# An encoder with 32 experts per layer: down weights in a ring of their own, one more megabyte ahead, row operations on GpSimd

## The chip, the core and the metric

The kernel runs on one core of a Trainium2 chip. The metric is the device time of one execution in microseconds (us); the time before is the median of three runs. A profile of one further execution shows what each engine and each DMA queue did. Engines are TensorE (PE; its weight loads as PEld), VectorE (DVE), ScalarE (ACT), GpSimd (POOL) and SyncE (SP), which here only issues transfers.

## What is computed

A trunk of two layers over 256 tokens of width 1024, all in float32. Each layer mixes tokens by four branches behind one input projection and then runs a mixture of 32 experts, of which each token takes two:

```python
h = layer_norm(x, emb_ln_g, emb_ln_b)
for l in range(DEPTH):                                   # 2 layers
    mix = token_mixing(h, ...)                           # 4 branches, gates, output projection
    h = layer_norm(ALPHA * h + mix, ln1_g[l], ln1_b[l])
    ffn = hierarchical_moe(h, ...)                       # top-1 group, then top-2 experts of 32
    h = layer_norm(ALPHA * h + ffn, ln2_g[l], ln2_b[l])

def expert_block(xb, e):
    return (silu(xb @ w_gate[e]) * (xb @ w_up[e])) @ w_down[e]   # 1024x512, 1024x512, 512x1024
```

Every expert's three matrices are 2 MB each (a megabyte, MB, is 2^20 bytes where tiles are counted), so a layer reads 192 MB for its experts, whatever the tokens choose.

## The kernel before

**Weights as a stream.** `weight_sources` lists every weight of both layers in the order of use. `load_weight` takes the next megabyte of that list and loads it, on SyncE's queue, into a buffer of the pool that it is given; `take` hands a source's tiles out, and its `free(i)` calls `load_weight` with the pool of the buffer just used up. So a freed buffer at once asks for the next megabyte, and the requests go out in the order in which SyncE's program has them. A request waits for the engine that last read the buffer.

**The buffers.** A buffer holds 128 partitions of 8 KB, 1 MB. `rawp` has 8 for the whole run. `rawb` has 4 and is opened late in the mixing (at the third branch). In the expert stage the space of the mixing's split weights becomes a further ring: `open_ring`, a step of the hand-written order in `output_and_route`, opens `rawc` with 5 buffers and loads them. `rawd` adds one when routing has ended. That is 18 megabytes ahead of the first expert. Only `rawp` may load for the next layer: for the other pools `load_weight` returns (L186).

**An expert's tiles.** The gate and up weights of an expert are four tiles (kind "pair": a half of gate, a half of up, and again), the down weight two (kind "down", 1 MB each, 8 KB pieces), listed one expert later than its pair, as it is used. The last expert's down weight comes as two column halves of four small transfers each (kind "halves").

**The expert loop** (`moe`, L926 to L965). For each expert p there are twelve steps s. Steps 0 to 7 are the gate and up products of p, two tiles in steps 0 to 3 and two in steps 4 to 7; each pair of tiles is freed after its fourth step. Steps 8 to 11 are the down product of expert p-1, each tile freed after two steps. Between them, by the table `STEPS`, stand the evacuation of p's products (`evacuate`, after step 7), their transposes, silu, and `combine` of p-2 in step 9, and `weigh` of p-1 in step 11; gathers of the next four experts' tokens stand in step 9 too. After the loop the last expert's down product runs by halves, and the layer norm follows. The order on each engine is as written there (`manual_schedule`).

**Small tiles.** `t4` has 6 buffers of 4 KB per partition, `t2` 8 buffers of 2 KB. The selection matrices `g` of the gathers stand in `t4`.

**The start.** The two rows of the embedding norm (`load_rows`) are turned into columns by TensorE and copied by ScalarE (`turn_rows`, L311 to L318). `enter_mixing` computes the norm's statistics, issues `FILL[0]` = 28 filling products on TensorE (`keep_busy`, L356; each is two passes in the trace), normalises and transposes. `turn_rows` stands outside the part whose order is written by hand.

**The whole-row operations.** `finish_h` (L380 to L385) multiplies the normalised rows by the norm's gain and adds its offset, two operations for each of two row tiles of 128x1024, on VectorE, in the mixing of each layer. The next reader is the residual addition after the output product.

Of the kernel before, what the change touches and what calls it, by code (L numbers as in the profile page):

```python
# [10 lines left out]
F32 = mybir.dt.float32  # L11
# [18 lines left out]
FILL = (28, 16)  # L30
G = 2
# [75 lines left out]

class Kernel:
# [19 lines left out]
    def open_ring(self):  # L128

        self.close_side()  # L130
        self.side = [self.tc.tile_pool(name=f"rawc{self.layer}", bufs=RAW[2] * 2 // G + 1, side="right", reuse_waits="tile")]
        self.rawc, = (p.__enter__() for p in self.side)
        for _ in range(RAW[2] * 2 // G + 1):
            self.load_weight(self.rawc)

    def close_side(self):
        for p in self.side[::-1]:
            p.__exit__(None, None, None)
        self.side, self.rawc = [], None
# [6 lines left out]
    def weight_sources(self):  # L146
        a = self.a
        for l in range(self.depth):
            w = a["w_in"][l].rearrange("(k p) c -> p k c", p=128)
            d = COL_DIL  # L150

            def cols(*starts, w=w):
                return [(w[:, :, s:s + 256], 256) for s in starts]

            yield l, [(w[:, :, d:d + 512], 512)]
            yield l, [(w[:, :, d + 768:d + 1280], 512)]
            yield l, [(w[:, :, d + 1536:d + 2048], 512)]
            yield l, cols(d + 512, d + 1280)
            yield l, cols(d + 2048, 512)
            yield l, [(w[:, :, 0:512], 512)]  # L160
            yield l, [(w[:, :, COL_DIFF:COL_DIFF + 512], 512)]
            yield l, [(w[:, :, COL_DIFF + 512:COL_DIFF + 1024], 512)]
            yield l, [(a["const_big"][:, :2048].rearrange("p (k c) -> p k c", k=4), 512)]
            wb = a["w_branch"][l]
            for n in BRANCH_ORDER:
                for h in range(2):
                    s = COL_GATE + n * D + h * 512
                    yield l, [(w[:, :, s:s + 512], 512)]
                yield l, [(wb[n].rearrange("(k p) d -> p k d", p=128), 1024)]
            wo = a["w_out"][l].rearrange("(k p) d -> p k d", p=128)  # L170
            for h in range(2):
                yield l, [(wo[:, :, h * 512:(h + 1) * 512], 512)]
            for e in range(N_EXP + 1):
                if e < N_EXP:
                    yield l, [(a[name][l, e].rearrange("(f p k) c -> p f k c", f=2, k=4), 512)
                              for name in ("expert_w_gate", "expert_w_up")], "pair"
                if e:
                    src = a["expert_w_down"][l, e - 1].rearrange("(h p k) d -> p h k d", h=2, k=2)
                    yield l, [(src, D)], "halves" if e == N_EXP else "down"

    def load_weight(self, pool):
# [4 lines left out]
        if self.ahead is None or (pool in (self.rawb, self.rawc, self.rawd) and self.ahead[0] > self.layer):  # L186
            return
# [4 lines left out]
        if kind:  # L192
# [6 lines left out]
            elif kind == "down":  # L199
                t = pool.tile([128, 2, 2, 512], F32, tag="raw", name="raw")  # L200
                nc.sync.dma_start(t.rearrange("p k f c -> p k (f c)"), blocks[0][0][:, q])
            else:
                t = pool.tile([128, 4, 2, 256], F32, tag="raw", name="raw")
                src = blocks[0][0].rearrange("p h k (f i c) -> p h k f i c", f=2, i=2)
                for k in range(4):
                    nc.sync.dma_start(t[:, k], src[:, k // 2, k % 2, :, q])
# [13 lines left out]
        if self.part == parts:  # L220
            self.ahead = None

# [157 lines left out]
    def finish_h(self, *v):  # L380

        g, b = (self.broadcast(x) for x in v)
        for T in range(2):
            self.nc.vector.tensor_mul(self.h[T], self.h[T], g)
            self.nc.vector.tensor_add(self.h[T], self.h[T], b)  # L385


    def run(self):
        tc, nc, a = self.tc, self.nc, self.a
        with ExitStack() as ctx:  # L390
# [3 lines left out]
            self.rawb = self.rawc = self.rawd = None  # L394
# [20 lines left out]
            for n, w in CONST:  # L415
# [5 lines left out]
            self.turn_rows(self.load_rows([a[n].rearrange("(o d) -> o d", o=1) for n in ("emb_ln_g", "emb_ln_b")], 1,  # L421
                                          nc.scalar), 0)
# [15 lines left out]
            with tc.manual_schedule():  # L438
                for T in range(2):
# [356 lines left out]
    def moe(self, l):  # L796
        tc, nc, a, c = self.tc, self.nc, self.a, self.c
        mm, t2, t4, t8 = self.mm, self.t2, self.t4, self.t8
        with ExitStack() as ctx:
# [9 lines left out]
            def slots(e0, T):  # L809

                if T == 0:
                    gs[e0] = t4.tile([128, 2, batch, CAP], F32R, tag="t4", name="g")
# [61 lines left out]
            def evacuate(e):  # L874
                st["h", e] = t2.tile([128, 512], F32, tag="t2", name="hid")
                nc.scalar.copy(st["h", e].rearrange("q (h k p) -> q h p k", h=2, k=2),  # L876
                               gu.rearrange("q (h p k) -> q h p k", h=2, k=2))
# [45 lines left out]
            with tc.manual_schedule():  # L923
                self.load_weight(self.rawd)
                nc.vector.tensor_copy(meta[:, :, :, 1], gates)
                for p in range(N_EXP):  # L926
# [4 lines left out]
                    for s in range(12):  # L931
                        if s == 0:
                            tiles, _, free = self.take() if p else ahead
                        if s == 8 and p:
                            tiles, _, free = self.take()
# [19 lines left out]
                        elif p:  # L955
                            down(p - 1, s - 8, tiles[s // 2 - 4][:, s % 2], dn)
                            if s % 2:
                                free(s // 2 - 4)
# [104 lines left out]
    def output_and_route(self, l, rp, route, meta, slots, gather, gathered, begin):  # L1063
# [180 lines left out]
        bks(1)  # L1244
        starts(0, 1)
# [78 lines left out]
    def overflow(self, l, rp, route, sel, gates, count, xh, xl, acc):  # L1324
# [17 lines left out]
        with tc.For_i(0, n, 1):  # L1342
# [18 lines left out]
            xs = t4.tile([128, 8, CAP], F32, tag="t4", name="oxs")  # L1361
# [68 lines left out]
```

## Time and profile before

| | us |
|---|---|
| median of 3 runs (lowest to highest) | 1532.85 (1529.71 to 1535.23) |
| the profiled execution | 1530.08 |
| its span, first to last instruction | 1528.0 |
| TensorE busy | 1467.8 (96%) |
| VectorE, ScalarE busy | 571.0, 468.7 |
| GpSimd busy | 0.2 (4 memsets) |
| HBM read | 498.65 MB, 328 GB/s over the span |

The share of busy time is a mean over stages with different limits. The first layer's mixing runs to about 314 us, its experts from there to about 756, the second layer's mixing to about 1063 and its experts to about 1507; the last norm and the output end the span. A busy TensorE is not one at its peak, since the ends of its products are modelled.

### The profile page before, as it was taken

What the parts mean: (1) busy time and instruction counts of PE and PEld (TensorE: products, weight loads), DVE (VectorE), ACT (ScalarE), POOL (GpSimd) and SP (SyncE); (2) the same over time, 40 slices, a digit from 0 to 9 for tenths busy, and PEclk for the clock granted to TensorE, in tenths of its full rate; (3) what the DMA queues carried; (4) which work ended last, traced back from release to release, by engine and by line L of the source; (5) the groups of instructions that cost most, each with busy time, mean ns of one, the idle gap of its engine ahead of it and who ended that gap; (6) DMA issues with size and microseconds to landing.
All of it is one profiled execution on the core that took longest, in us unless ns stands there. A gap on an engine that the chain in (4) does not pass through costs nothing. (4 is left out here: it accounts for less than half of the span.)

```text
span 1528.0 us, 21590 instructions
## 1 busy us (share of the span) xinstructions
PE 1467.8 (96%) x8848; PEld 896.1 (59%) x8848; DVE 571.0 (37%) x1202; ACT 468.7 (31%) x764; POOL 0.2 (0%) x4
## 2 busy tenths in 40 slices
PE   8989999999999999999899999999999999999995
PEld 7777899844444444444378778997444444444432
DVE  5477765721111111111176766665111111111103
ACT  5445555521111111111264555454111111111111
POOL 0000000000000000000000000000000000000000
PEclk9989999999999999999999999999999999999998
DMA  9744485679999999999988336746999999999996
GB/s 334 230 167 138 136 303 195 249 306 419 420 420 419 420 420 419 419 420 421 391 246 308 111 111 214 252 167 254 395 420 420 419 420 420 419 420 420 421 420 217
DMA packets 121658, 501.16 MB, mean 328 GB/s; under 512 B 23050, under 2 KB 35786, under 8 KB 72660
## 3 DMA queue, kind: packets, MB, share of 16 engines
q1 hardware_dynamic: 121248, 499.14, 83.8%
q8 instruction: 72, 1.18, 0.3%
q10 hardware_dynamic: 308, 0.60, 0.1%
q14 instruction: 30, 0.25, 0.0%
HBM read 498.65 MB, written 2.00 MB: 328 GB/s over the span
## 5 line engine op out<-in xcount | busy, mean ns | idle before, releaser
L854 PE MATMUL bank<-raw,xs 128*64 128x512 f32 x2048 | 481.7, 595 | 20.0 <-DMA raw<-in_expert_w_up_dram 19.9
L854 PEld LDWEIGHTS bank<-raw,xs 128*64 128x64 f32 x2048 | 166.3, 137 | 302.2 <-issue 239.5
L896 PE MATMUL bank<-raw,act 128*64 128x512 f32 (+1 forms) x1056 | 261.0, 586 | 0.0
L239 DVE TENSOR_TENSOR wl<-raw,wh 128x1024 fp32r<-128x1024 f32 x159 | 192.6, 1222 | 113.7 <-ACT wh L234 110.0
L876 ACT COPY hid<-bank 128x512 f32<-128x512 f32 x64 | 68.3, 1067 | 457.9 <-PE bank L854 457.9
L234 ACT CAST wh<-raw 128x1024 fp32r<-128x1024 f32 x159 | 165.6, 1050 | 136.6 <-PE mm L484 60.6
L831 DVE COPY xs<-bank 128x256 f32<-128x256 f32 x116 | 43.9, 420 | 421.9 <-PE bank L822 421.9
L484 PE MATMUL mm<-hth,wh 128*128 128x256 f32 x576 | 162.8, 283 | 0.0
L484 PE MATMUL mm<-hth,wl 128*128 128x256 f32 x576 | 162.4, 282 | 0.0
L484 PE MATMUL mm<-htl,wh 128*128 128x256 f32 x576 | 162.2, 282 | 0.0
L896 PEld LDWEIGHTS bank<-raw,act 128*64 128x64 f32 x1056 | 78.4, 136 | 130.8 <-issue 124.6
L908 DVE SCALAR_TENSOR_TENSOR y<-bank,tg,y 128x512 fp32r<-128x512 f32 (+1 forms) x66 | 48.5, 735 | 178.0 <-ACT y L907 178.0
L484 PEld LDWEIGHTS mm<-hth,wh 128*128 128x128 f32 x576 | 109.1, 189 | 2.4 <-issue 2.2
L484 PEld LDWEIGHTS mm<-htl,wh 128*128 128x128 f32 x576 | 109.2, 190 | 1.1 <-issue 0.8
L484 PEld LDWEIGHTS mm<-hth,wl 128*128 128x128 f32 x576 | 109.1, 189 | 1.0 <-issue 0.8
L907 ACT ACTIVATE y<-bank,tg 128x512 fp32r<-128x512 f32 (+1 forms) x66 | 44.5, 674 | 166.2 <-PE bank L896 166.2
L465 PE MATMUL mm<-wh,hth 128*128 128x512 f32 x220 | 72.7, 402 | 1.0 <-ACT hth L300 1.0
L465 PE MATMUL mm<-wl,hth 128*128 128x512 f32 x220 | 71.7, 401 | 0.0
L465 PE MATMUL mm<-wh,htl 128*128 128x512 f32 x220 | 70.2, 398 | 0.0
L822 PEld LDWEIGHTS bank<-g,xh 128*128 128x128 f32 x240 | 36.9, 192 | 50.9 <-issue 50.9
L888 ACT ACTIVATE act<-bank 128x256 f32<-128x256 f32 x64 | 24.6, 385 | 127.7 <-PE bank L882 125.5
L822 PE MATMUL bank<-g,xh 128*128 128x256 f32 x240 | 55.0, 311 | 3.7 <-DVE g L813 3.7
(228 smaller groups left out, 1453.6 us busy)
## 6 DMA issues: line engine op xcount, KB each, us to landing
raw<-in_expert_w_gate_dram SPq DMA_DIRECT2D x128, 1024.0 KB, 19.9
raw<-in_expert_w_up_dram SPq DMA_DIRECT2D x128, 1024.0 KB, 19.9
raw<-in_expert_w_down_dram SPq DMA_DIRECT2D x124, 1024.0 KB, 19.9
raw<-in_w_in_dram SPq DMA_DIRECT2D x56, 1024.0 KB, 7.7
raw<-in_w_in_dram SPq DMA_DIRECT2D x16, 512.0 KB, 11.1
raw<-in_w_branch_dram SPq DMA_DIRECT2D x8, 1024.0 KB, 6.3
raw<-in_w_out_dram SPq DMA_DIRECT2D x8, 1024.0 KB, 8.1
raw<-in_expert_w_down_dram SPq DMA_DIRECT2D x16, 256.0 KB, 13.8
```

Of the source, the lines that this page charges most:

```text
L234: self.nc.scalar.copy(hi, s)
L239: self.nc.vector.tensor_sub(lo, s, raw(hi))
L465: nc.tensor.matmul(ps[T], s[:, kk, T * 128:(T + 1) * 128], m[:, k], stop=kk == 7 and s is stat[1], start=kk == 0 and s is stat[0] and m is wh)
L484: nc.tensor.matmul(ps[j // 2][:, j % 2], m[:, k, j * 128:(j + 1) * 128], s[:, kk], start=j % 2 == 0 and kk == 0 and m is wh and s is hth, ...
L822: nc.tensor.matmul(ps[:, o:o + 256], (xh, xl)[i][:, T, k], gs[e0][:, T], start=i == 0 and T == 0, stop=i == 1 and T == 1)
L831: (nc.scalar.copy if on_scalar else nc.vector.tensor_copy)(xs[e0 + 2 * i][:, :, 2 * j:2 * j + 2], ps[:, 2 * i:2 * i + 2])
L854: nc.tensor.matmul(gu[half[i]], x, w, start=k == 0, stop=k == 7)
L876: nc.scalar.copy(st["h", e].rearrange("q (h k p) -> q h p k", h=2, k=2), gu.rearrange("q (h p k) -> q h p k", h=2, k=2))
L888: nc.scalar.activation(st["a", e], fv[:, :, 0], AF.Silu)
L896: nc.tensor.matmul(ps[half[f], :w.shape[2]], st["a", e][:, k], w[:, f], start=k == 0, stop=k == 3)
L907: nc.scalar.activation(yh, ps, AF.Copy, scale=g)
L908: nc.vector.scalar_tensor_tensor(yl, ps, g, raw(yh), op0=ALU.mult, op1=ALU.subtract)
```

## The change

The down weight of an expert becomes one transfer of 2 MB, 128 pieces of 16 KB, into a ring of its own: `rawc` now has 2 such buffers, and a new pool `rawe` has 1 buffer of 1 MB for the common stream. `open_ring` loads the down weights of experts 0 and 1, then one tile into `rawe`. In the loop, `load_down` for expert p+1 follows step 11 of p. The list of `weight_sources` keeps the pairs and the last expert's halves alone. A new step `load_loose` loads one tile of a pair (the nineteenth megabyte) into two buffers of `t4`, once per layer, and such a tile is not refilled. For that, `g` and one tile of the overflow loop move from `t4` to `t2`. With 16 KB pieces, partition q holds rows 4q to 4q+3 of the down matrix, so the index layouts of `evacuate` and of the halves follow. `finish_h` goes to GpSimd. At the start `turn_rows` moves into the hand-written order, ahead of the statistics, and the filling products go from 28 to 22.

```diff
-FILL = (28, 16)
+FILL = (22, 16)
...
+class Two:
+
+    def __init__(self, *tiles):
+        self.tiles = tiles
+
+    def __getitem__(self, i):
+        return self.tiles[i[1] // 2][:, i[1] % 2]
...
-        self.side = [self.tc.tile_pool(name=f"rawc{self.layer}", bufs=RAW[2] * 2 // G + 1, side="right", reuse_waits="tile")]
-        self.rawc, = (p.__enter__() for p in self.side)
-        for _ in range(RAW[2] * 2 // G + 1):
-            self.load_weight(self.rawc)
+        self.side = [self.tc.tile_pool(name=f"{n}{self.layer}", bufs=b, side="right", reuse_waits="tile")
+                     for n, b in (("rawc", RAW[2] // G), ("rawe", 1))]
+        self.rawc, self.rawe = (p.__enter__() for p in self.side)
+        self.downs = {}
+        for e in range(RAW[2] // G):
+            self.load_down(e)
+        self.load_weight(self.rawe)
...
+    def load_down(self, e):
+
+        t = self.rawc.tile([128, 4, 2, 512], F32, tag="down", name="raw")
+        self.nc.sync.dma_start(t.rearrange("p k f c -> p (k f c)"),
+                               self.a["expert_w_down"][self.layer, e].rearrange("(p k) d -> p (k d)", k=4))
+        self.downs[e] = t
...
+    def load_loose(self):
...
+        ts = [self.t4.tile([128, 2, 512], F32, tag="t4", name="raw") for _ in range(2)]
+        for i, t in enumerate(ts):
+            self.nc.sync.dma_start(t, blocks[q % 2][0][:, q // 2, 2 * i:2 * i + 2])
+        self.loaded[-1][0].append((Two(*ts), None, False))
+        self.part += 1
...
-            self.nc.vector.tensor_mul(self.h[T], self.h[T], g)
-            self.nc.vector.tensor_add(self.h[T], self.h[T], b)
+            self.nc.gpsimd.tensor_mul(self.h[T], self.h[T], g)
+            self.nc.gpsimd.tensor_add(self.h[T], self.h[T], b)
...
             with tc.manual_schedule():
+                self.turn_rows(rows, 0)
...
-                    gs[e0] = t4.tile([128, 2, batch, CAP], F32R, tag="t4", name="g")
+                    gs[e0] = t2.tile([128, 2, batch, CAP], F32R, tag="t2", name="g")
...
-                nc.scalar.copy(st["h", e].rearrange("q (h k p) -> q h p k", h=2, k=2),
-                               gu.rearrange("q (h p k) -> q h p k", h=2, k=2))
+                nc.scalar.copy(st["h", e].rearrange("q (k p) -> q p k", k=4), gu.rearrange("q (p k) -> q p k", k=4))
...
-                        if s == 8 and p:
-                            tiles, _, free = self.take()
...
-                            down(p - 1, s - 8, tiles[s // 2 - 4][:, s % 2], dn)
-                            if s % 2:
-                                free(s // 2 - 4)
+                            down(p - 1, s - 8, self.downs[p - 1][:, s - 8], dn)
+                            if s == 11 and p + RAW[2] // G < N_EXP:
+                                self.load_down(p - 1 + RAW[2] // G)
...
         bks(1)
+        S("loose", self.load_loose)
         starts(0, 1)
...
-            xs = t4.tile([128, 8, CAP], F32, tag="t4", name="oxs")
+            xs = self.t2.tile([128, 8, CAP], F32, tag="t2", name="oxs")
```

## Rows read from the trace of the kernel before

**Rows 1.** Stretches (us from:to, length, busy us of each engine (count), TensorE clock, DMA share, GB/s).

```profile
298.00:314.00 16.00, 14.76 (x105) 11.14 (x103) 10.61 (x54) 8.81 (x18) 0.00 (x0) 1.00 0.43 180
322.00:580.00 258.00, 257.97 (x1440) 111.49 (x1439) 46.79 (x112) 41.78 (x59) 0.00 (x0) 1.00 1.01 419
580.00:756.00 176.00, 165.76 (x865) 74.34 (x864) 23.40 (x55) 24.93 (x35) 0.00 (x0) 1.00 1.01 416
1046.00:1062.00 16.00, 15.63 (x114) 12.08 (x113) 10.77 (x55) 9.26 (x19) 0.00 (x0) 1.00 0.62 258
```

**Rows 2.** Timeline (start us, us, engine, line, operation, tiles), TensorE's first weight wait.

```profile
581.55 1.50 PE L854 MATMUL bank<-raw,xs 128*64 128x512 f32 x5 [0.69 <-DMA raw<-in_expert_w_up_dram]
```

**Rows 3.** The chain that ended last (start us, us, what), around one expert.

```profile
1126.75 6.87 PE bank L854 x32
1133.62 1.72 PE bank L896 x8
1135.34 1.15 PE bank L822 x8
...
1139.92 6.87 PE bank L854 x32
```

**Rows 4.** DMA from 400 to 700 us: packets, MB, share; issues, KB, us to landing.

```profile
q1 hardware_dynamic: 17267, 125.74, 101.0%
...
raw<-in_expert_w_down_dram SPq DMA_DIRECT2D x40, 1024.0 KB, 19.9
```

**Rows 5.** Waits of SyncE's queue: who, for what, us in total, times, longest.

```profile
SPq L198 <- DMA raw<-in_expert_w_down_dram: 174.0, 85, 2.6
```

**Rows 6.** Timeline of ScalarE, the weigh that follows each layer's loop.

```profile
756.44 0.69 ACT L907 ACTIVATE y<-bank,tg 128x512 fp32r<-128x512 f32 x1 [2.62 <-PE bank L896]
...
1506.92 0.69 ACT L907 ACTIVATE y<-bank,tg 128x512 fp32r<-128x512 f32 x1 [2.63 <-PE bank L896]
```

**Rows 7.** DMA issues from 752.3 to 752.9 us, then from 1492.5 to 1493.2.

```profile
raw<-in_expert_w_down_dram SPq DMA_DIRECT2D x1, 256.0 KB, 5.8
...
raw<-in_expert_w_down_dram SPq DMA_DIRECT2D x1, 256.0 KB, 12.9
```

**Rows 8.** Stretches, one behind the first layer's experts.

```profile
768.00:772.00 4.00, 4.00 (x23) 2.99 (x22) 3.90 (x6) 4.00 (x9) 0.00 (x0) 1.00 1.04 386
```

**Rows 9.** DMA queue from 205 to 215 us (2 KB pieces), 776 to 779 (1 KB).

```profile
q1 hardware_dynamic: 1671, 3.32, 97.3%
...
q1 hardware_dynamic: 1040, 1.03, 108.0%
```

**Rows 10.** Timeline of the start: TensorE, ScalarE, VectorE, TensorE.

```profile
3.67 8.41 PE L356 MATMUL spare<-cs 128*128 128x128 f32 x48 [3.67 <-DMA cs<-in_const_small_dram]
...
12.70 0.17 ACT L318 COPY cols<-mm 128x16 f32<-128x16 f32 x1 [9.95 <-PE mm L317]
12.77 0.48 ACT L272 ACTIVATE w<-mv,eps 128x1 f32<-128x1 f32 x2
...
9.88 0.33 DVE L271 BATCH_NORM_AGGREGATE mv<-st 128x2 f32<-128x12 f32 x2
...
15.07 1.09 PE L367 MATMUL at<-cs,h 128*128 128x128 f32 x8 [1.32 <-ACT h L292]
```

**Rows 11.** Timeline around the first layer's whole-row operations: VectorE, ScalarE, TensorE.

```profile
80.55 2.35 DVE L384 TENSOR_TENSOR h<-h,ln 128x1024 f32<-128x1024 f32 x2
...
85.09 0.21 DVE L619 RECIPROCAL m<-m 128x1 f32<-128x1 f32 x2
...
80.05 0.72 ACT L618 ACTIVATE p<-p,m 128x512 f32<-128x512 f32 x1 [1.61 <-DVE m L617]
80.68 0.19 ACT L618 ACTIVATION_READ_ACCUMULATOR p<-p,m 128x1 f32 x1
...
85.82 1.97 PE L623 MATMUL at<-cs,p 128*128 128x128 f32 x8 [6.55 <-DVE p L620]
```

**Rows 12.** Stretches: behind that gap, and around the second layer's whole-row operations.

```profile
84.00:88.00 4.00, 2.18 (x10) 2.18 (x11) 4.00 (x9) 1.35 (x2) 0.00 (x0) 0.50 0.12 44
...
816.00:820.00 4.00, 4.00 (x19) 3.21 (x18) 4.00 (x4) 2.46 (x6) 0.00 (x0) 1.00 1.04 389
```

## What the change was predicted to do

> **What bounds the kernel now.** I read the busy time by stretch first. In the long expert stretches the DMA engines have no free time from start to end (share 1.01, 419 and 416 GB/s) [rows 1]. TensorE is full in the first part (257.97 of 258.00 us) and not in the second (165.76 of 176.00). So the DMA queue sets the pace of the whole stretch, and TensorE lives from what was loaded ahead until that is used up; its first wait for a weight stands at 581.55 us [rows 2]. The stretches just ahead of the experts are the other way round: DMA share 0.43 and 0.62 with TensorE nearly full [rows 1]. There the ring is full and a megabyte more would be free.
>
> The pace of one expert comes from two views. TensorE: from 1126.75 to 1139.92 us is 13.17 us, of which 6.87 are the gate and up products (steps 0 to 7) and 1139.92 - 1133.62 = 6.30 are steps 8 to 11 with the down product [rows 3]. Without the gather for later experts (1.15) steps 8 to 11 take about 5.2. DMA: 6 transfers of 1.0486 MB at 419 to 420 GB/s are 2.50 us each, 15.0 us [rows 1, 4]. TensorE gains 1.8 us per expert until the stock is gone.
>
> Two more things matter about the queue. A transfer takes 19.9 us from issue to landing [rows 4], so eight of 2.5 us are under way; and SyncE stands waiting for older transfers to land, 174.0 us in 85 waits on one line alone [rows 5]. Requests go out strictly in SyncE's program order, and behind the eight under way further ones stand ready. A request that is made late is served late.
>
> **Part 1, the down weights leave the common ring.** Before, the order of loading is the order of use, over all 18 buffers. Now gate and up tiles run 14 buffers ahead (3.5 experts), while down weights run two experts ahead: that of expert p+1 is asked for at the end of step 11 of p and needed at step 8 of p+2. TensorE alone takes 13.17 + 6.87 = 20.0 us between the two. The transfer itself is 5.0 us, so 15.0 us of queue may stand ahead of it. The queue grows by 1.8 us per expert, so after some 8 to 12 experts the down weight is late and TensorE runs at the pace of DMA, with gate and up weights of later experts lying unused. DMA never idles (10 MB stay requested behind each down weight), so the middle of the stretch costs nothing. The price falls due at the end, where TensorE still has work on tiles that have long landed.
>
> Second layer, by hand. Last requests in order: two tiles of expert 31, its four-part down halves, down 29, down 30. Before, the fourth of the eight small transfers is issued at about 1492.9 and lands 12.9 us later, 1505.8 [rows 7]; four more of 0.26 MB in 1 KB pieces, at the 1.03 MB in 3 us of [rows 9] 0.76 us each, end at about 1508.8. The bytes are the same but for one megabyte loaded ahead (part 2): the last, now down 30, lands at 1508.8 - 2.5 = 1506.3, and down 29 at 1501.3. TensorE waits for down 29 at step 8 of p=30, then has 5.2 + 6.87 + 5.2 = 17.3 us to the end of the loop: 1518.6. Before, the loop ended where ScalarE's weigh starts, 1506.9 [rows 6]. Cost +11.7 us.
>
> First layer: tiles of the next layer use the eight buffers of one pool as they come free. Tile n goes where tile n-14 was, so in p=29 three of four freed buffers are of that pool, and three next-layer megabytes are asked for ahead of down 30. At 386 GB/s these take 2.72 us each [rows 8]. Before, the last half lands at 752.5 + 5.8 = 758.3 [rows 7]; down 30 now lands at 758.3 - 2.5 + 8.2 = 764.0, and 5.2 us of TensorE follow: 769.2 against 756.4 [rows 6]. Cost +12.8 us. The next-layer tiles that came early give nothing back, since TensorE is full right after the boundary (4.00 of 4.00 us) [rows 8].
>
> **Part 2, the nineteenth megabyte** is 2.5 us per layer, already taken off in both sums; it lies in the slack ahead of the experts [rows 1]. Were that slack gone, it would be worth nothing.
>
> **Part 3, 16 KB pieces.** The trace of before has none on a data queue. 8 KB pieces: 1.01 x 16 x 300 us over 3 x 40 x 128 pieces is 315 ns each [rows 4]. 2 KB pieces: 0.973 x 16 x 10 us over 1671 is 93 ns [rows 9]. A line through both gives 36 to 37 ns per KB and 19 ns per piece, so two 8 KB pieces (630) become one of about 611: 3% off the down weights at the best, 0.15 us per expert, 4.5 us per layer over some 30 experts. The 2 KB stretch was not saturated all through, which makes the fixed part too large; the other end is no change. Nothing excludes a loss, so that end stands 1% below zero (+1.5 us per layer). I take 1.8 us per layer, nearer to none, as the 8 KB row is the nearest. The Trainium skill ("DMA: Bandwidth & Descriptors", section "Where 436 GB/s comes from") puts a ceiling of 435 GB/s on the fabric; by it the down weights would gain at most the same 3.5%, and no run here shows that ceiling.
>
> One transfer in place of two saves nothing in itself: the share is 1.01 with eight under way [rows 4].
>
> **Part 4, start.** ScalarE sits 9.95 us before it copies the embedding rows at 12.70, and the square root of the first norm is queued behind that at 12.77, though its input stood at 9.88 + 0.33 = 10.2; from there 2.30 us lead to the transposes at 15.07 [rows 10]. The copy waits for TensorE, which runs 48 filling passes first (8.41 us, 175 ns each). Moved ahead, the turn (eight small passes, by the length of eight filling ones at most 1.2 us; I take 0.6) runs once the rows are there, which I put at about 4.8, a little behind the constants of 3.67; 44 passes more (7.7 us) end at 13.1, while the norm is ready at 12.5. Gain 15.07 - 13.1 = 1.9 us; bounds 0 (rows late) and 2.6.
>
> **Part 5, GpSimd.** In the first layer the four whole-row operations hold VectorE from 80.55 to 85.09, while the reciprocal that follows could have run when ScalarE was through, at 80.68 + 0.19 = 80.87; TensorE sits 6.55 us idle for it [rows 11]. Gain 4.2 us. After the gap the granted clock was 0.50, the lower of the two levels (1.2 GHz) [rows 12]; with a gap of 2.4 us it may stay up, but VectorE is full there (4.00 of 4.00) and sets the pace, so I add 0.2: 4.4 us. Bounds 2 (other VectorE work moves in) and 8 (the slow clock also goes). In the second layer TensorE is full around the same operations (4.00 of 4.00) [rows 12]: nothing. On GpSimd no row shows their duration; below, it is the 1.2 us each of VectorE (2.35 for two), above I allow ten times that. The rows are read again only by the residual addition after the output product, at the end of the mixing, so even 50 us are covered; without that cover each would stand in the path whole. The Trainium skill ("GPSIMD Engine Reference", section "Engine selection") speaks against the move, with GpSimd about 2x slower than VectorE for two inputs. By that the four take about 10 us in place of 4.9, an estimate; the sum would be the same, and no run here shows it yet.
>
> The remaining edits (two tile tags to a smaller ring of eight, three index layouts) keep the instruction counts. At worst ScalarE's evacuation waits for a buffer, under its cover of one half down product; bounds 0 and 2 us per layer; I take 0.
>
> **Sum**, against the profiled execution (1530.1 us; span 1528.0 and 2.1 around it): 1530.1 - 1.9 - 4.4 + (12.8 - 1.8) + (11.7 - 1.8) = 1544.7. That run lies 2.8 under the median of the three, so the forecast is 1547 us, about 0.9% slower.
>
> **Rivals.** *The down weights are never late* (the queue ahead of them stays under 15 us, or the transfers overtake). Then only bytes and the early gains count: 1532.9 - 6.3 - 2 x (2.5 + 1.8) = 1518, faster. For it: TensorE has 20 us of cover; against it: requests served in order 19.9 us after issue with more waiting to be issued [rows 4, 5]. It decides for "faster" if the wait stays under about 3 us per layer at the end. Chance 0.13.
> *Large pieces and early gains are both at their upper ends*: 4.5 per layer and 2.6 + 8: 1532.9 - 10.6 + (12.8 - 4.5) + (11.7 - 4.5) = 1538, the edge of no change; with the tail some us shorter it lies inside. Chance 0.08.
> *The change does less than it says*: no early gain, no faster pieces, a buffer wait: 1532.9 + 24.5 + 1 = 1558. Chance 0.05, on the slower side.
> *A fixed cost per transfer in series* would give 2 us for each of 60 pairs made one, by the Trainium skill's fit in the same DMA page ("Anatomy of one DMA"): an estimate of 120 us off. With the engines' share at 1.01 [rows 4] that time isn't there; chance under 0.01, within the first rival.
>
> **How the numbers follow.** Forecast, late down weights: 0.74. Measurement tells 0.3% (4.6 us) from no change. Faster 0.14, within 0.3% 0.08, slower 0.78. Range: the forecast's own bounds, 1538 to 1558, widened below to 1534 for the second rival; the first stays outside.
>
> **What would show it.** In the changed profile TensorE's wait ahead of the down product, for the down weight, begins near expert 10 in place of expert 20, about 1.8 us each time, while DMA stays at 1.01; the gate and up products never wait; the last down weight of each layer lands after the last expert's halves; the loop ends some 11 and 10 us later, counted from each expert stretch's start. The start shows transposes near 13 us, the idle time at 80 us shrinks from 6.55 to about 2.4. It is wrong if the wait falls on gate or up tiles, or if DMA idles between experts (then it is worse), or if the mean rate exceeds 430 GB/s.

## The result, and the profile after

The changed kernel takes 1568.91 us (median of four, 1566.37 to 1570.29) against 1531.28 for the kernel before on the same chip: ratio 1.0245, interval 1.0223 to 1.0267. It is slower, as predicted, but by 37.6 us where 14 were forecast, and above the range. Its profiled execution took 1567.76 us, with a span of 1565.6 against 1528.0.

First the ends of the two expert loops, ScalarE's weigh that follows each; it answers to [rows 6] (timeline: start us, us, engine, line, operation, tiles, idle before and its releaser).

```profile
775.01 0.69 ACT L931 ACTIVATE y<-bank,tg 128x512 fp32r<-128x512 f32 x1 [2.64 <-PE bank L920]
...
1544.68 0.69 ACT L931 ACTIVATE y<-bank,tg 128x512 fp32r<-128x512 f32 x1 [2.62 <-PE bank L920]
```

The first is 18.6 us later than before, the second 37.8; nothing is lost behind that. The same instruction in both traces, at more places, divides the loss:

| place | before | after | shift |
|---|---|---|---|
| first layer, attention transposes behind the whole-row operations (PE L623, now L648) | 85.82 | 79.08 | -6.7 |
| a later transpose of the mixing (L664, now L689) | 117.70 | 111.83 | -5.9 |
| first product of expert 0 (L854, now L879) | 309.46 | 308.33 | -1.1 |
| first product behind the overflow loop (L822, now L847) | 314.87 | 320.98 | +6.1 |
| end of the first expert loop | 756.44 | 775.01 | +18.6 |
| second layer, transposes of z (L562, now L587) | 795.04 | 824.17 | +29.1 |
| first product of expert 0 | 1058.41 | 1082.88 | +24.5 |
| weigh of expert 0 | 1086.31 | 1114.54 | +28.2 |
| end of the second expert loop | 1506.92 | 1544.68 | +37.8 |

The expert loops lose 12.5 and 9.5 us from their own starts, which the prediction has. The rest it does not have: 7.2 us at the entry of the first overflow loop, 10.5 between the first loop's end and the second layer's transposes, 3.7 from the second layer's first product to its first weigh. TensorE's waits name most of these (who, for what, us in total, times, longest):

```profile
PE bank L920 <- DMA raw<-in_expert_w_down_dram: 54.2, 38, 3.4
PE at L587 <- DVE z L574: 8.4, 1, 8.4
...
PE bank L879 <- DVE g L838: 5.3, 1, 5.3
PE bank L879 <- SPq L1365: 4.9, 1, 4.9
```

Before, the first place was a wait for up tiles, 19.9 us in 24 times; now no expert product waits for a gate or up tile, and the down product waits 38 times. The second line is new, one wait of 8.4 us. The last two are the two entries of the overflow loop (L1365). The first of the 38 waits, at expert 10:

```profile
469.62 1.94 PE L920 MATMUL bank<-raw,act 128*64 128x512 f32 x8 [0.56 <-DMA raw<-in_expert_w_down_dram]
```

The stretches, as in [rows 1]:

```profile
298.00:314.00 16.00, 11.08 (x81) 9.36 (x81) 9.01 (x49) 7.89 (x17) 0.00 (x0) 0.98 0.82 333
314.00:320.00 6.00, 5.27 (x13) 1.57 (x14) 0.70 (x2) 0.00 (x0) 0.00 (x0) 0.50 0.48 178
322.00:580.00 258.00, 247.51 (x1408) 106.28 (x1408) 43.84 (x106) 39.58 (x57) 0.00 (x0) 1.00 1.00 416
580.00:775.00 195.00, 177.59 (x958) 72.10 (x956) 27.28 (x64) 27.38 (x39) 0.00 (x0) 0.98 1.01 414
```

TensorE was busy 14.76 us from 298 to 314 and is now busy 11.08, and behind that it runs at half its clock. In the long stretch it is no longer full (247.51 of 258), while DMA is, as before.

**GpSimd.** VectorE, then GpSimd, then TensorE, in the second layer:

```profile
813.50 2.48 DVE L569 TENSOR_TENSOR rope<-z,cs 128x128 f32<-128x128 f32 x1
815.91 3.36 DVE L264 TENSOR_TENSOR wl<-raw,wh 128x1024 fp32r<-128x1024 f32 x1
819.19 2.42 DVE L570 TENSOR_TENSOR z<-z,cs 128x128 f32<-128x128 f32 x1
821.65 2.38 DVE L574 TENSOR_TENSOR z<-z,rope 128x64 f32<-128x64 f32 x2
...
813.38 4.80 POOL L409 TENSOR_TENSOR h<-h,ln 128x1024 f32<-128x1024 f32 x2 [736.53 <-ACT wh L259]
818.14 5.67 POOL L410 TENSOR_TENSOR h<-h,ln 128x1024 f32<-128x1024 f32 x2
...
824.17 1.51 PE L587 MATMUL at<-cs,z 128*128 128x128 f32 x6 [8.40 <-DVE z L574]
```

The forms of L569 and L570 last 0.28 us each a little earlier in the same trace, L574 0.22 and L264 1.22. Here each of these (of L574 the first) lasts 2.0 to 2.2 us longer. GpSimd's four end at 815.8, 818.2, 821.5 and 823.8; VectorE's small ones end 0.1 to 0.2 us behind one of them, L264 1.1 us behind one, nearly its own length: the engines take turns by whole instructions. The Trainium skill ("SBUF — State Buffer", section "SBUF: two separate sides") calls the port pair that the two share an exclusive lock held for the whole instruction; the trace agrees, at 2.2 us a turn.

**The entry of the overflow loop.** Its tokens never overflow here, so no pass runs. TensorE around it, in the first layer:

```profile
308.33 1.07 PE L879 MATMUL bank<-raw,xs 128*64 128x512 f32 x2
314.73 6.32 PE L879 MATMUL bank<-raw,xs 128*64 128x512 f32 x14 [5.32 <-DVE g L838]
320.98 0.51 PE L847 MATMUL bank<-g,xh 128*128 128x256 f32 x2
```

Before, all 16 passes of `begin` stood ahead of the loop, in one run of 3.65 us from 309.46. Now one product of eight (two passes) stands ahead and seven behind; TensorE idles for 5.32 us and does the rest at half clock. Which side they stand on is chosen when the program is laid out (the loop is not in the part ordered by hand), and it flipped with `load_loose`: in all four versions with that step at its place (the change and runs 3, 4 and 5) seven of the eight stand behind, and without it, or with it later, all eight stand ahead (but in run 9, where they are put behind by hand). SyncE, meanwhile, resets the semaphores of its transfers at the loop, and for each it waits until that transfer has landed. The last two are the nineteenth megabyte's (DMA issues from 295 to 298 us: KB each, us to landing):

```profile
raw<-in_expert_w_up_dram SPq DMA_DIRECT2D x2, 512.0 KB, 16.3
```

Issued at 295.32 and 296.73, they land at 311.7 and 312.9, while SyncE stands at the loop from 309.0; it asks for the next tile at 314.62, in place of 313.72, and for the one after that at 320.16, in place of 314.11, since its buffer comes free only with the delayed products. In the second layer the same stall ends at 1087.55 and TensorE resumes at 1088.82.

**TensorE's pace in the mixing** moves by itself. Two adjacent groups of three equal products, in the first and in the second layer of the changed trace:

```profile
182.28 0.28 PE L803 MATMUL mm<-y,wl 128*128 128x256 f32 x1
182.40 0.40 PE L803 MATMUL mm<-y,wh 128*128 128x256 f32 x2
182.63 0.28 PE L803 MATMUL mm<-y,wl 128*128 128x256 f32 x1
...
960.17 0.28 PE L803 MATMUL mm<-y,wl 128*128 128x256 f32 x1
960.28 0.39 PE L803 MATMUL mm<-y,wh 128*128 128x256 f32 x2
960.51 0.28 PE L803 MATMUL mm<-y,wl 128*128 128x256 f32 x1
```

0.35 us per three against 0.34: a product every 118 or every 113 ns, at a granted clock of 1.00 both times, from about 120 us ahead of the experts to their start. One pace in place of the other is worth about 5 us per layer. The kernel before has 113 in its first layer and 118 in its second, the changed one the reverse, so the two cancel (+4.8 and -4.6 of the shifts above). Below, a profile's stretches are compared with this in mind.

### The profile page after: what moved, and what is told of

It reads as the page before. It is cut to its first block, busy times and chain, and to the rows that moved or that the text cites. A ratio compares the mean times of both kernels' runs of the same rounds, so it can differ in the third digit from the quotient of the medians.

```text
span 1565.6 us, 21467 instructions
## 1 busy us (share of the span) xinstructions
PE 1460.2 (93%) x8836; PEld 872.8 (56%) x8836; DVE 576.3 (37%) x1194; ACT 467.8 (30%) x764; POOL 23.0 (1%) x12
## 5 line engine op out<-in xcount | busy, mean ns | idle before, releaser
L879 PE MATMUL bank<-raw,xs 128*64 128x512 f32 x2048 | 461.1, 597 | 10.2 <-DVE g L838 5.3
L879 PEld LDWEIGHTS bank<-raw,xs 128*64 128x64 f32 x2048 | 149.0, 138 | 294.0 <-issue 284.1
L920 PE MATMUL bank<-raw,act 128*64 128x512 f32 (+1 forms) x1056 | 249.7, 594 | 54.4 <-DMA raw<-in_expert_w_down_dram 54.2
L264 DVE TENSOR_TENSOR wl<-raw,wh 128x1024 fp32r<-128x1024 f32 x159 | 196.1, 1244 | 120.6 <-ACT wh L259 115.9
L920 PEld LDWEIGHTS bank<-raw,act 128*64 128x64 f32 x1056 | 70.9, 136 | 194.8 <-issue 193.1
L931 ACT ACTIVATE y<-bank,tg 128x512 fp32r<-128x512 f32 (+1 forms) x66 | 44.5, 675 | 169.8 <-PE bank L920 169.8
L847 PEld LDWEIGHTS bank<-g,xh 128*128 128x128 f32 x240 | 36.2, 188 | 47.1 <-issue 47.1
L915 DVE TENSOR_TENSOR act<-act,bank 128x256 f32<-128x256 f32 x64 | 27.0, 421 | 78.2 <-ACT act L912 73.0
```

The lines of the kernel that those rows point to most:

```text
L264: self.nc.vector.tensor_sub(lo, s, raw(hi))
L847: nc.tensor.matmul(ps[:, o:o + 256], (xh, xl)[i][:, T, k], gs[e0][:, T], start=i == 0 and T == 0, stop=i == 1 and T == 1)
L879: nc.tensor.matmul(gu[half[i]], x, w, start=k == 0, stop=k == 7)
L920: nc.tensor.matmul(ps[half[f], :w.shape[2]], st["a", e][:, k], w[:, f], start=k == 0, stop=k == 3)
L931: nc.scalar.activation(yh, ps, AF.Copy, scale=g)
```

## Experiments: the down ring

**1. The ring alone**, on the kernel before: `load_down`, `rawc`, `rawe` and the index layouts of the change, and neither the nineteenth megabyte nor the edits at the start nor GpSimd.

> The kernel before with only the down ring (2 MB transfers in 16 KB pieces, two buffers), so without the nineteenth megabyte, GpSimd or the edits at the start. Theory, late down weights: by the prediction's own terms 12.8 + 11.7 - 2 x 1.8, and 2 x 2.5 for the megabyte that is not there, 1531.3 + 25.9 = 1557 us. Rival, the ring costs little and the loss lies in the other edits: 1531 to 1535.

Measured: 1558.64 us, ratio 1.0173 (1.0124 to 1.0221). From the weigh of expert 0 to the loop's end the layers take 434.8 and 434.5 us, against 420.8 and 420.6 before: 14.0 and 13.9. TensorE's first wait, and the end of the first loop:

```profile
465.05 1.94 PE L920 MATMUL bank<-raw,act 128*64 128x512 f32 x8 [1.48 <-DMA raw<-in_expert_w_down_dram]
...
770.79 0.69 ACT L931 ACTIVATE y<-bank,tg 128x512 fp32r<-128x512 f32 x1 [2.61 <-PE bank L920]
```

The prediction's terms for this part, without the megabyte, were 13.5 and 12.4: 0.5 and 1.5 short. The wait begins at expert 10, as it said.

**2. A deeper ring.** Three down weights in halves in place of two whole ones, paid for with two tile buffers of the common stream:

```diff
+        t = (self.rawd if n % 6 == 5 else self.rawc).tile([128, 2, 2, 512], F32, tag="raw", name="raw")
+        src = self.a["expert_w_down"][self.layer, e].rearrange("(p h k) d -> p h (k d)", h=2, k=2)
...
-                            if s == 11 and p + RAW[2] // G < N_EXP:
-                                self.load_down(p - 1 + RAW[2] // G)
+                            if s % 2 and n + 6 < 2 * (N_EXP - 1):
+                                self.load_half(n + 6)
```

> The kernel of the run with the ring alone, with a down ring of three weights in place of two: six halves of 1 MB in 8 KB pieces, five in the ring's space and the sixth behind the overflow loop, paid for with the two tile buffers there; 18 MB in all, as before. A half is requested again as soon as the one in its place is used up, 33 us of TensorE's time ahead of its need in place of 20. Theory, the down weights were late only because they were requested later than the 22 to 23 us that a request takes in the queue: TensorE's waits begin near expert 19 as in the trace before, each layer's experts take 421 to 423 us in place of 434.8, and the time is 1531 to 1537 us against 1558.6. Rival, a second ring in the queue costs by itself (order of service, more buffers waited for): 1550 to 1559.

Measured: 1530.64 us, ratio 1.001 (0.9982 to 1.0038). The layers take 420.6 and 420.5 us, and the first wait falls on an up tile, at the expert and nearly the time of the trace before (581.55) [rows 2]:

```profile
582.51 1.50 PE L878 MATMUL bank<-raw,xs 128*64 128x512 f32 x5 [0.68 <-DMA raw<-in_expert_w_up_dram]
```

So the whole loss of the ring is its depth: how long ahead a down weight is requested, not that there are two rings. That is shown: this run also loads in halves of 1 MB, but halves in a ring of two weights leave the loss (run 3).

**3. Pieces of 8 KB.** The changed kernel with each down weight as two transfers into the same buffer:

```diff
+        src = self.a["expert_w_down"][self.layer, e].rearrange("(p h k) d -> p h (k d)", h=2, k=2)
+        for h in range(2):
+            self.nc.sync.dma_start(t[:, 2 * h:2 * h + 2].rearrange("p k f c -> p (k f c)"), src[:, h])
```

> The changed kernel, with each down weight as two transfers of 1 MB in 8 KB pieces into the same 2 MB buffer. Theory of the price of a piece: the pace of an expert that waits for DMA goes from 14.87 us back to the 14.94 of the trace before, over some 18 to 20 experts per layer, so 1.3 to 1.8 us per layer: 1571.5 to 1572.5 us against 1568.9. Rival, the size of the pieces is of no weight: the pace stays at 14.87.

Measured: 1562.87 us, ratio 1.0194 (1.0159 to 1.0228): not slower than the change, perhaps a little faster. The rate does fall, from 423 GB/s at 600 to 720 us to 420:

```profile
600.00:720.00 120.00, 109.54 (x612) 45.90 (x610) 18.53 (x44) 16.82 (x24) 0.00 (x0) 1.00 1.01 420
```

and an expert there takes 14.95 us in place of 14.85. But TensorE's first wait comes two experts later:

```profile
498.33 1.94 PE L921 MATMUL bank<-raw,act 128*64 128x512 f32 x8 [1.23 <-DMA raw<-in_expert_w_down_dram]
```

(469.62 in the changed kernel), and the first layer's experts take 433.1 us, as with large pieces (433.2); the second layer's take 431.4 in place of 430.1. The profiled execution took 1567.22 us, as long as the change's, so it does not show where the median's 6 us lie. Two reasons for the later wait are visible. With halves the product starts when the first has landed. And a transfer lands 19.9 us after its issue, as in [rows 4], where the 2 MB transfers take 23.0: eight transfers are under way however large they are (the loop's entry resets eight of their semaphores), so larger ones make a longer queue.

```profile
raw<-in_expert_w_down_dram SPq DMA_DIRECT2D x20, 2048.0 KB, 23.0
```

(the changed kernel, 400 to 700 us). The gain of the pieces is real, 0.1 us per expert; in the first layer one transfer in place of two gives it back, in the second 1.2 us of it stay. The rival with 2 us per transfer is out: this run has 62 transfers more than the change and is not slower. The Trainium skill ("DMA: Bandwidth & Descriptors", section "Anatomy of one DMA") gives that fit for transfers that GpSimd issues, and these are SyncE's.

**4. The down weights in ScalarE's queue**, from expert 2 on (`nc.scalar.dma_start` in `load_down`).

> The changed kernel, with the down weights from expert 2 on requested by ScalarE, so in a queue of their own and not behind the tiles that SyncE has requested. Theory, late down weights are late because they are served in turn behind some 20 us of older requests: in their own queue they share the engines at once, TensorE's waits for them (54.2 us in 38) shrink to a few, and the ends of the layers lose the 12.5 and 9.5 us that the changed trace has there: about 1547 us against 1568.9, and TensorE waits for gate or up tiles instead. Rival, the pair of buffers itself is too short (a buffer is free for less time than a transfer of 2 MB takes in any queue): the waits stay and the time is 1566 to 1570.

Measured: 1570.21 us, ratio 1.0247 (1.0216 to 1.0279), no gain. Yet the transfer itself is served early:

```profile
raw<-in_expert_w_down_dram ACTq DMA_DIRECT2D x20, 2048.0 KB, 12.7
```

What is late is the request, and what is queued behind it:

```profile
472.81 0.39 ACT L912 ACTIVATE act<-bank 128x256 f32<-128x256 f32 x1 [2.17 <-PE bank L906]
479.29 0.33 ACTq L193 DMA_DIRECT2D raw<-in_expert_w_down_dram  x1
479.68 0.69 ACT L931 ACTIVATE y<-bank,tg 128x512 fp32r<-128x512 f32 x1 [6.48 <-PE bank L879]
```

Before it may issue, a transfer waits for its completion semaphore, whose earlier user is one of SyncE's tiles (ScalarE waits 239.1 us in all for up tiles ahead of L931); the weigh stands behind the request, and TensorE behind the weigh. Neither theory is right as written: the queue's length was cured, and the wait moved to ScalarE. Run 2 settles what this one leaves.

## Experiments: GpSimd

**5. GpSimd in the first layer only**, in the changed kernel: `e = self.nc.vector if self.layer else self.nc.gpsimd` in `finish_h`.

> The changed kernel, with the whole-row operations of the second layer back on VectorE (those of the first layer stay on GpSimd). Theory, the two engines take turns: in the changed trace three small VectorE operations at 813.5 to 823.9 us last 2.2 to 2.5 us each in place of 0.2 to 0.3, beside GpSimd's four, and TensorE waits 8.4 us for the last of them. That wait goes and the second layer's mixing is 9 to 10 us shorter: 1559 us against 1568.9. Rival, TensorE would have waited there for something else that came late (the broadcast rows land at 813 to 816): the time stays at 1569.

Measured: 1561.84 us, ratio 1.0208 (1.0168 to 1.0248), some 6 us less than the change, though the two intervals overlap. VectorE at the same place:

```profile
809.19 0.28 DVE L570 TENSOR_TENSOR rope<-z,cs 128x128 f32<-128x128 f32 x1
809.39 1.22 DVE L264 TENSOR_TENSOR wl<-raw,wh 128x1024 fp32r<-128x1024 f32 x1
810.53 2.36 DVE L410 TENSOR_TENSOR h<-h,ln 128x1024 f32<-128x1024 f32 x2
```

The rotation is short again and TensorE's wait there is 0.2 us. From the first loop's end to the first product behind the second overflow loop, 313.1 us stand against 318.7 in the changed kernel: 5.6 less, though at the slow pace (118) where that had the fast one (113); so some 10 us by the pace. Run 12, which also has VectorE in the second layer and runs at the fast pace there, gives it without that correction. Its end of the first loop, and its first product of expert 0 in the second layer:

```profile
766.18 0.69 ACT L933 ACTIVATE y<-bank,tg 128x512 fp32r<-128x512 f32 x1 [2.62 <-PE bank L922]
...
1063.39 1.94 PE L880 MATMUL bank<-raw,xs 128*64 128x512 f32 x8
```

297.2 us lie between them, against 307.9 in the changed kernel (775.01 to 1082.88): 10.7 less. The wait was GpSimd's.

**6. GpSimd in both layers, alone**, on the kernel before.

> The kernel before with the whole-row operations on GpSimd in both layers and nothing else. Theory, the first layer gains the 4 us of VectorE's time at 80 us, and in the second GpSimd starts as soon as the broadcast rows land, beside the rotation of queries and keys, and holds VectorE up by 2.2 us per operation: TensorE waits 4 to 9 us for it, so 1531 to 1536 us against 1529 to 1531. Rival, without the ring the rows land at another moment and nothing meets: 1526.

Measured: 1532.76 us, ratio 1.003 (1.0005 to 1.0055). The median alone doesn't show that GpSimd costs anything: its 3.5 us are about the 3 us that the second overflow loop takes here for its code (last section). The trace does. GpSimd and TensorE in the second layer:

```profile
810.42 4.71 POOL L384 TENSOR_TENSOR h<-h,ln 128x1024 f32<-128x1024 f32 x2 [734.28 <-DVE wl L239]
...
815.36 1.51 PE L562 MATMUL at<-cs,z 128*128 128x128 f32 x6 [3.87 <-DVE z L549]
```

From the first loop's end to expert 0 of the second layer it takes 304.0 us, against 297.1 in run 10 at the same pace, where VectorE has this layer: some 7 us, without any ring. And in the first layer its gain does not last: TensorE is 4.4 us ahead at 81 us, 0.4 at 117, and 1.8 behind at expert 0, at the same pace as before.

## Experiments: the loop's entry and the nineteenth megabyte

**7. Without the nineteenth megabyte** (the step `loose` taken out of the changed kernel).

> The changed kernel without the nineteenth megabyte. Theory, the overflow loop's entry waits until every transfer under way has landed, and with the nineteenth megabyte seven of the eight first products of expert 0 stand behind that loop in TensorE's order: the expert stretches start 6.8 and 3.7 us later than the mixing before them explains (10.5 in all). Without it the products stand ahead of the loop again and the transfers land 2.5 us sooner: 10.5 us less, and up to 5.0 more at the ends of the two layers, where the megabyte is missing: 1558.4 to 1563.4 us. Rival, the later start is only the longer landing of large pieces, and the order is of no weight: the megabyte's loss outweighs, 1569 to 1571.

**8. The nineteenth megabyte later** (`self.load_loose()` moved behind `self.overflow(...)`).

> The changed kernel with the nineteenth megabyte requested right behind the overflow loop in place of ahead of it. Theory of the loop's entry: the 10.5 us are saved as without the megabyte, and since DMA stands idle behind the loop's entry for some 5 us, the megabyte is loaded and keeps its worth of 2.5 us per layer: 1558.4 us, that is 5 below the run without it. Rival, the megabyte was never worth anything, since the down weights and not the gate and up tiles are what TensorE waits for: the same time as without it.

Measured: 1561.79 us, ratio 1.0201 (1.0157 to 1.0245), and 1563.4 us, ratio 1.0209 (1.0163 to 1.0254). In both, all eight products stand ahead of the loop again. Run 8 around it:

```profile
306.10 3.65 PE L879 MATMUL bank<-raw,xs 128*64 128x512 f32 x16
311.49 0.51 PE L847 MATMUL bank<-g,xh 128*128 128x256 f32 x2 [1.74 <-DVE g L838]
```

From 306.10 to 311.49 are 5.4 us, as before (5.4), against 12.65 in the changed kernel: 7.3 us in the first layer. In the second, from the first product to the weigh of expert 0 as in the table above, 30.6 against 31.7 (before: 27.9): only 1.1 of the 3.7 come back, since some 3 us of code take their place (last section). The megabyte's worth is read from 7 against 8: the layers take 435.1 and 433.0 us without it, 434.8 and 431.0 with it, so 0.2 and 2.0 us in place of 2.5 each. The medians do not tell the two runs apart, as run 8's rival has it, and they can't be divided further: the second layer's wait for VectorE (4.3 and 6.3 us, against 8.4) and the pace differ too.

**9. The eight products behind the loop, by hand**, on the kernel before (`begin()` called behind `overflow`).

> The kernel before, with nothing changed but the place of expert 0's first eight products: they are put behind the overflow loop by hand (in the changed kernel seven of them stand there). Theory, those products are the cover under which the loop is entered (SyncE and TensorE spend some 3 to 5 us on it, though the loop runs no pass): behind it TensorE stands still for 5 us and then does them at the lower clock, so each expert stretch starts 5 to 7 us later and, since every later request waits for TensorE, ends as much later: 1539 to 1543 us against 1529.3. Rival, the order is of no weight: DMA, idle at the loop in any case, sets the end of each layer, and only the late landing of the changed kernel's transfers cost time: 1528 to 1532.

Measured: 1540.19 us, ratio 1.0069 (1.0042 to 1.0097), 11.6 us over the 1528.57 beside it. TensorE's last gather ends at 314.7, and then:

```profile
320.68 5.13 PE L854 MATMUL bank<-raw,xs 128*64 128x512 f32 x11 [5.96 <-issue]
```

In the second layer the idle time is 4.8 us. SyncE is through with its resets at 316.7, at most 0.2 us of waiting among them, so every transfer had landed: the order alone is enough for the loss. What fills the 6 us, mostly one branch of 3.7 us, is told in the last section.

## Experiments: what is left

**10. The early edits alone**: on the kernel before, the rows turned early, 22 filling products, and GpSimd in the first layer.

> The kernel before with the edits at the start (turned rows earlier, 22 filling products) and with GpSimd's whole-row operations in the first layer alone; no ring, no nineteenth megabyte. Theory, the changed trace is 5.9 us ahead at 112 us, and only later losses hide it: the kernel is 6 us shorter, 1525 us. Rival, a later stage gives the gain back (DMA sets the pace of the experts): 1530 to 1532. Rival, GpSimd holds VectorE up in the first layer too: within 2 us of 1531.

**11. The same with the nineteenth megabyte** behind the overflow loop.

> The run above with the nineteenth megabyte as well, requested behind the overflow loop, in the kernel before's common stream. Theory, in a stream in the order of use one megabyte more ahead is worth its 2.5 us per layer at the end: 1520 us. Rival, DMA is what is short behind the loop, and a megabyte requested there only moves the others back: 1525, as without it.

Measured: 1525.4 us, ratio 0.9988 (0.9962 to 1.0014), and 1525.12 us, ratio 0.997 (0.9948 to 0.9993). The first is not told apart from the kernel before, nor the second from the first. TensorE reaches expert 0 at 305.4 against 309.5, both at the fast pace, so 4.1 us of the 6.3 arrive there. The megabyte shortens the experts by 0.3 and 2.2 us (420.7 and 420.6 to 420.4 and 418.4). The second of these is the one version here that is faster than the kernel before clear of noise.

**12. Both losses taken out of the change**: runs 5 and 8 together; the ring stays.

> The changed kernel with both of the smaller losses taken out: GpSimd's whole-row operations in the first layer only, and the nineteenth megabyte requested behind the overflow loop; the down ring stays. Theory, the losses are separate and add up: 1568.9 - 10 (TensorE's wait beside GpSimd and its after-effects, with TensorE's pace evened out) - 10 (later expert starts) = 1549 us, near the 1547 that was predicted without those two. Rival, they overlap, since whatever comes early waits at the loop or for DMA: 1556 to 1562, as either run alone.

Measured: 1554.85 us, ratio 1.0178 (1.0145 to 1.0212), between the two theories. In its trace: 3.9 us earlier at expert 0, experts 13.7 and 11.8 longer than before, the stretch between the layers' experts 1.6 shorter at the faster pace; together 20, and the span is 20.5 longer. So the losses add up, but the megabyte behind the loop is worth less than ahead of it, and 2.4 of the 6.3 us of early gain are gone before the experts.

## Why the prediction was right, and where it was not

**The ring** (part 1, with parts 2 and 3 in its sums) was predicted as 11.0 and 9.9 us per layer and cost 12.5 and 9.5. The mechanism is the one named: waits for down weights from expert 10 (469.62 us), none for gate or up tiles, DMA full throughout, the last down weight landing last (1531.7, the last half at 1521.9), and run 2 takes it away by depth alone. The first layer's term is 1.5 short: 0.5 of that stands in run 1 already, and the rest is the megabyte, worth 1.6 to 1.9 there and not 2.5 (433.2 us against 434.8 in run 1 and 435.1 in run 7). The second layer's 9.5 for 9.9 is partly luck: without the megabyte the term is 1.5 short (run 1), and the changed kernel makes up for it in a stretch that starts late, for a reason that no run shows.

**The pieces** were taken as 1.8 us per layer. The pace gives about 0.1 us per expert, the same size; that one transfer "saves nothing in itself" was too kind, since it costs about as much again in the first layer, by a queue of 23.0 us in place of 19.9 and by the wait for all of it.

**The start** came as told, by luck: transposes at 13.05 for 13.1, though the rows landed at 5.8 and not 4.8, the turn took 0.98 and not 0.6, and the 44 filling passes 6.5 and not 7.7. (Eight filling passes of 175 ns are 1.4 us, where the prediction has 1.2.) **GpSimd in the first layer** too, at its place: the idle time of 6.55 us [rows 11] is 2.37 now, though the clock fell in spite of that (granted 0.65 from 80 to 84 us). But what was booked as a gain to the end is gone 35 us later when GpSimd comes alone (run 6): TensorE stands still for another 1.9 us until 90.5, for a split weight of VectorE's (L239), and its granted clock is 0.70 from 92 to 96 where it was 1.00. Both early edits together bring expert 0 forward by 4.1 (run 10).

**Step that failed, part 5.** "TensorE is full around the same operations: nothing", and 50 us of GpSimd "are covered". The step costed GpSimd's own time and who reads its result, and not who else is held while it runs. Before, VectorE had these four operations in its own order, behind the rotation (from 814.6 us, where the transposes of z end at 810.1); GpSimd has no such order and starts when the broadcast rows land, in the midst of the rotation that TensorE waits for. 10.5 us in place of 0 up to those transposes, the wait of 8.4 being most of it. At the same pace it is 10.7 up to expert 0 (run 12). The Trainium skill ("GPSIMD Engine Reference", section "Engine selection"), which the prediction cited for GpSimd's speed, was right on that (2.4 us each against 1.2 for VectorE), and speed was not the point.

**Step that failed, parts 2 and the sum.** The nineteenth megabyte was laid "in the slack ahead of the experts". The row with the slack (share 0.43) was read as free time up to the experts, but the loop's entry stands in it, at which no transfer may be under way: the last one landed at 305.4 before and lands at 312.9 now, with SyncE at the loop from 309.0. The loop stood in the kernel; its entry was no term of the sum. It cost 7.2 and 3.7 us, by the order of `begin` (run 9) and by the landing; how these two divide the 7.2 is not shown, since each alone can fill it. In the second layer TensorE waits for SyncE, and SyncE for the landing.

Put together: 0.4 + 1.5 - 0.4 us on what was predicted, 7.2 + 3.7 + 10.5 on what was not, and 0.2 from the paces make 23.1, the distance between the forecast's 14.6 and the trace's 37.7.

## What to carry to other kernels

Give a ring of its own only to a stream whose request stands further ahead of its need than the queue is long, and count that queue in transfers: larger ones lengthen it. Before moving work to GpSimd, ask which VectorE operations will run beside it and who waits for those, and keep it in an order that holds it away from them. A loop that runs no pass is still a place at which transfers must have landed and engines meet: see that there is work ahead of it on the engine that matters, and look there first when a step added elsewhere changes the order.

## What was not expected of the hardware

Two paces of TensorE at one granted clock, 113 and 118 ns per product of 256 columns: of the 28 mixing stretches in the 14 profiles, 18 end at 113. The change from 118 comes at about the same instructions each time, or not at all; what decides it is open. It makes some 5 us per layer; how much of the spread between the times of one kernel it makes was not measured, as only one execution of each is profiled.

TensorE's way past the overflow loop takes about 3 us more or less by the code that it needs. In the kernel before its branch there lasts 0.3 and 0.6 us in the two layers. In each of the other 13 profiles it lasts 3.3 to 4.1 us in one of the two: in the second layer where the eight products stand ahead of the loop (8 profiles), in the first where seven or eight of them stand behind it (5, the changed kernel among them). In each of these 13 an instruction transfer of 16 KB starts 1.0 to 1.7 us into that branch. In run 1 (1075.1 to 1078.8 us; queue, packets, MB, share of the engines):

```profile
q8 instruction: 1, 0.02, 2.1%
```

TensorE then goes on at 1079.97, after 5.04 us of idle time; in the kernel before such a transfer ran 3.7 and 1.7 us ahead of its two branches. The Trainium skill ("Runtime: NRT & Kernel Launch", section "Instruction fetch mechanics") says that a taken branch to code that isn't loaded waits for it; the trace agrees, at about 3 us. So products ahead of the loop hide this as well, and the second layer's 3 us in runs 1, 2, 6 to 8 and 10 to 12 belong to no edit's own work. Why the code was there in time in both layers of the kernel before is open.
